# Splits of weights and operands queued on ScalarE behind a visit's last exponential, in an attention loop that runs beside large products

## The chip, the core and the metric

The kernel runs on one core of a Trainium2 chip. The core has a matrix engine (TensorE, PE in the profile), a vector engine (VectorE, DVE), a scalar engine (ScalarE, ACT), GpSimd (POOL) and a sync engine (SyncE, SP) that issues most of the DMAs. Each engine has its own list of instructions and they wait for one another through semaphores. The metric is the device time of one execution in microseconds (us). Three runs of the kernel before took 1274.01, 1275.73 and 1276.46 us, so its median is 1275.73 us.

## What is computed

One layer of a hybrid decoder, for 1024 tokens of width 1024, in float32. After a norm, one wide projection makes all inputs. One branch is a state-space scan (SSD), the other is attention with a forgetting gate; both pass through a product with a matrix of their own, are merged by sigmoid gates, and go through an output product and a norm. The part that matters here is the attention of 16 heads:

```python
def _forgetting_attention(q, k, v, log_f):
    seqlen = q.shape[2]
    scale = ATT_HEAD_DIM ** -0.5
    fcum = jnp.cumsum(log_f, axis=-1)
    outs = []
    for blk in range(seqlen // ATT_BLOCK):
        q0, q1 = blk * ATT_BLOCK, (blk + 1) * ATT_BLOCK
        s = jnp.einsum('bhqd,bhkd->bhqk', q[:, :, q0:q1], k[:, :, :q1]).astype(jnp.float32) * scale
        s = s + fcum[:, :, q0:q1, None] - fcum[:, :, None, :q1]
        ...
        prob = jax.nn.softmax(s, axis=-1)
        outs.append(jnp.einsum('bhqk,bhkd->bhqd', prob.astype(v.dtype), v[:, :, :q1]))
...
merged = jax.nn.sigmoid(g_ssm) * p_ssm + jax.nn.sigmoid(g_att) * p_att
out = jnp.einsum('bld,de->ble', merged, w_out)
```

## The kernel before

All large products are computed by a scheme of Strassen's kind: each pair of output units is made of seven smaller products, called steps 1 to 7. A step is twelve matmuls of 128x128 by 128x512 in two halves of six. There are twelve because each operand is kept as two pieces, a high piece that is rounded and a low piece that is the rest, and high times high, high times low and low times high are summed for each of four blocks. The weight of a step has the tile `wop`. `Pair.split` makes it: ScalarE copies the raw block (or a sum of blocks) into the high piece (L349), and VectorE subtracts that from the raw block into the low piece (L350). The other operand, one of x0 to x6, has tiles such as x5h (high) and x5l (low); `Operands.split` makes them block by block, the high on ScalarE (L275, L278) and the low on VectorE (L276, L279). A low piece always needs its high piece.

`Stream` holds the list of all steps and runs it in halves. At each step `Stream.ahead` calls `prepare` for the step three places further on, which splits its weight, and `Operands.some` fetches and splits operand blocks of pairs still to come.

The attention runs in 48 visits, eight pairs of heads times six groups of rows and keys, and halves of the product stream are run in between so that TensorE has work while the softmax is computed. Each visit `m` goes in this order: `scores` (two rounds `u` of twelve matmuls into PSUM tiles s, VectorE's row minimum nm with bias, L1505, and ScalarE's exponential ex, L1509, each four times per visit); `weighted` for the visit before (matmuls into av); `free`; the work deferred from the visit before, such as `second` (x at L1594, then y at L1595, for which y was loaded by a DMA at L1569); a number `ahead` of product halves; `turned` (TensorE transposes the exponentials into PSUM tiles pt; ScalarE, at L1548, or VectorE, at L1546, evacuates them into p); and a number `behind` of halves. The PSUM tiles s and pt share one set of four banks, so the scores of a visit wait for the evacuations of the one before. During `behind` the operand work is held back (`hold`) and done by `release` in the next visit.

The order of each engine's list is set by a scheduler that estimates times. Blocks under `tc.high_priority()` come early, and instructions wrapped in `pin` keep the order in which the program wrote them. `tc.issue_after(i)` gives what is traced inside it an edge in the order of issue behind instruction `i`, on the engine of `i`, without a semaphore.

Other lines named below: L402 (`keep`) and L413 to L419 (`give`) take finished products out of PSUM; L629 and L644 apply tanh to gates, L645 and L1074 continue with them on VectorE; L1413, L1414 normalise; L1457, L1469 and L1470 form the attention output o and zr; L1373 is GpSimd's mask, L1432 a DMA of ScalarE.

Of the kernel before, what the change touches and what calls it, by code (L numbers as in the profile page):

```python
# [11 lines left out]
AF = mybir.ActivationFunctionType  # L12
# [74 lines left out]
def hybrid_layer(ctx: ExitStack, tc, a, out):  # L87

    nc = tc.nc
# [43 lines left out]
    def pin(op):  # L133
        return tc.keep_in_program_order(op)
# [326 lines left out]
    class Stream:  # L461
# [6 lines left out]
        def __init__(self, pairs, double, last):  # L468
            self.pairs = pairs
            for n, p in enumerate(pairs):  # L470
                p.bank, p.other = (pj, "be"[n % 2]), (pjx, "d") if n < double else (pj, "c")

                p.between = n < double or n >= last

            p, q, r = pairs[0:3]
            self.steps = [(p, 1), (q, 1), (p, 2), (q, 2)] + [(p, n) for n in (6, 5, 7, 4, 3)]
            self.steps += [(q, 6), (q, 5), (q, 7), (r, 1), (q, 4), (q, 3)]
            for n in range(2, last):
                p, nxt = pairs[n], pairs[n + 1]
                self.steps += [(p, i) for i in ((2, 6, 5, 7) if n < double else (6, 2, 7, 5))] + [(nxt, 1)]  # L480
                self.steps += [(p, 4), (p, 3)] if n + 1 < last else [(p, 3), (p, 4)]

            a, b, c, d, e, f, g, h = pairs[last:]
            self.steps += [(a, 5), (a, 6), (a, 7), (b, 1), (a, 2), (a, 4), (a, 3)]
            for p, nxt in ((b, c), (c, d), (d, e)):
                self.steps += [(p, 2), (p, 6), (p, 5), (p, 7), (nxt, 1), (p, 4), (p, 3)]
            self.steps += [(f, 1), (e, 2), (e, 6), (e, 5), (e, 7), (f, 2), (e, 4), (e, 3)]
            self.steps += [(f, 6), (f, 5), (f, 7), (g, 1), (f, 4), (f, 3)]
            self.steps += [(g, 2), (g, 6), (g, 5), (g, 7), (h, 1), (g, 4), (g, 3)]
            self.steps += [(h, 6), (h, 5), (h, 7), (h, 2), (h, 3), (h, 4)]  # L490
            self.following = {p: n.ops for p, n in zip(pairs, pairs[1:]) if n.ops is not p.ops}
            self.building = []
            self.chores, self.line = [], []
            self.held = None
            self.count = 0
            self.at = 0
            self.run = None
            self.waiting = []
            self.loads = [(p, names) for p in pairs for names in (("a11", "a12"), ("a21", "a22"))]
            self.loaded = []  # L500
            self.load_next()

        def load_next(self):
            p, names = self.loads.pop(0)
            p.load(names)
            if p.keys[0][0] != "merged":
                self.loaded += [(p, n) for n in names]

        def load_more(self):

# [14 lines left out]
                self.prepare(p, which)  # L525

        def prepare(self, p, which):
            p.prepare(which)
            self.load_more()

        def after(self, halves, fn):
# [3 lines left out]
        def half(self):  # L535
            if self.run is None:
                if self.at == len(self.steps):
                    return False
                p, which = self.steps[self.at]
# [12 lines left out]
            else:  # L552
# [3 lines left out]
                p, which = self.steps[self.at]  # L556
                if p in self.following:
                    ops = self.following[p]
# [4 lines left out]
                self.at += 1  # L563
            for ops in self.building:
                if self.held is None:
                    ops.some()
                else:
                    self.held.append(ops)
            for chores in (self.chores, self.line):
# [16 lines left out]
        def release(self):  # L586
            held, self.held = self.held or [], None
            for ops in held:
                ops.some()

        def do_chores(self):
            while self.chores:
# [734 lines left out]
    with tc.tile_pool(name="att", bufs=1, reuse_waits="tile", side="right") as ap, tc.tile_pool(  # L1327
# [148 lines left out]
        def scores(hp, g, u):  # L1476

            pair, h = GROUPS[g]
            i = pair[u]
# [20 lines left out]
            for e in range(2):  # L1500
                o = ex[:, e, u, 0:w]
                nm = hd.at(hd.nm, i, h, e)
                with tc.high_priority():
                    pin(
                        nc.vector.tensor_tensor_reduce(  # L1505
                            o, s[e][:, 0:w], fb[hp, h][:, e, 0:w], 1.0, 3.0e38, ALU.add, ALU.min, nm
                        )
                    )
                    pin(nc.scalar.activation(o, o, AF.Exp, scale=-1.0, bias=nm, accum_out=hd.at(hd.sm, i, h, e)))  # L1509

        def turned(hp, g, sent):

# [160 lines left out]
        def room(m):  # L1673

            share = weights[m // 6] * rooms[m % 6] if m < 6 * NK - 1 else 1.4
            to = stream.steps.index((ends[4], 6))
            n = round((2 * (to - stream.at) - (stream.run is not None)) * share / left[0])
            left[0] -= share
            if m == 6 * NK - 1:
                return n // 2, n - n // 2  # L1680
            behind = n // 2 if n > 3 else min(max(n - 1, 0), 1)
            return n - behind, behind

        made = []
        for m in range(6 * NK + 1):
# [9 lines left out]
            for hd, which in end(m - 1):  # L1695
                hd.free(which)
            if m == 6 * NK:
                stream.release()
                heads[NK - 1].out(2)
                break  # L1700
# [7 lines left out]
            for hd, which in end(m):  # L1708
                hd.settle(which)
            ahead, behind = room(m)  # L1710
            stream.halves(ahead)

            for hd, which in end(m):
                hd.scale(which)
# [78 lines left out]
```

## Time and profile before

| what | value |
|---|---|
| median of three runs | 1275.73 us |
| time of the profiled execution | 1273.87 us |
| its span | 1272.2 us |
| PE busy | 1246.1 us (98%) |
| VectorE busy | 1012.9 us (80%) |
| ScalarE busy | 794.3 us (62%) |
| GpSimd busy | 319.3 us (25%) |
| granted TensorE clock, mean | 0.999 |
| share of PE in the chain that ended last | 86% |

A line of the profile names the line of the program, the engine, the operation, the tile written and the tiles read, and how many of them; then busy time and the mean of one in ns; then the time for which the engine was idle just ahead of them, and what ended most of it. A line of the timeline starts with the start time and the duration in us; brackets at its end give an idle time before it and what ended it. In a line of waits, the engine and line that waited stand first, then what was waited for, and then the total in us, the number of waits and the longest.

### The profile page before, as it was taken

The numbers are of one execution on the slowest core, as the hardware profiler recorded it, in microseconds if no ns is written. First come the engines' busy times: TensorE is split into PE (matmuls) and PEld (weight loads), VectorE is DVE, ScalarE is ACT, GpSimd is POOL, SyncE is SP. The second block draws the span as 40 slices with busy tenths as digits, with TensorE's granted clock in tenths as the row PEclk, the third lists the DMA queues.
The fourth block names the chain that finished last, engine by engine and source line by source line (L and its number), as shares of the span: only waits on it lengthen the run. The fifth ranks groups of instructions, "written<-read, shape, count | busy, mean of one in ns | idle before, by whom it ended". The sixth has DMA issues, their size and how long they took to land.

```text
span 1272.2 us, 20822 instructions
## 1 busy us (share of the span) xinstructions
PE 1246.1 (98%) x6926; PEld 982.3 (77%) x6926; DVE 1012.9 (80%) x1994; ACT 794.3 (62%) x1737; POOL 319.3 (25%) x322
## 2 busy tenths in 40 slices
PE   5999999999999999999999999999999999999997
PEld 3678888888888888888887777777777777778886
DVE  7988886988888978997767676767789767886975
ACT  7745665556665765566555666666687666844753
POOL 4000440013400241115102124223112212356062
PEclk9999999999999999999999999999999999999999
DMA  8232452545436533744447576666687657766933
GB/s 300 69 120 76 146 162 88 191 152 182 138 101 215 175 127 117 219 146 140 142 149 252 162 228 212 217 214 218 232 286 263 224 184 249 249 221 199 364 110 105
DMA packets 152236, 233.56 MB, mean 184 GB/s; under 512 B 15201, under 2 KB 60737, under 8 KB 152129
## 3 DMA queue, kind: packets, MB, share of 16 engines
q1 hardware_dynamic: 136064, 196.08, 47.7%
q10 hardware_dynamic: 10560, 18.06, 3.8%
q0 software_dynamic: 5504, 18.09, 3.7%
q8 instruction: 54, 0.88, 0.3%
q14 instruction: 54, 0.43, 0.1%
HBM read 162.99 MB, written 72.34 MB: 185 GB/s over the span
## 4 chain that ended last, share of the span: by engine, by line
PE 86%; DMA 4%; DVE 4%; ACT 4%; issue 1%; SPq 0%; POOL 0%; DVEq 0%; ACTq 0%; POOLq 0%
PE pb L128 36%; PE pc L128 21%; PE pd L128 7%; PE av L128 5%; PE pt L131 5%; PE s L128 5%; PE yps L128 2%; PE st L128 1%; ACT ex L1509 1%; DMA xt<-in_x 1%; PE tr L131 1%; PE tr_v L131 1%; DMA v<-v_dram 1%; PE df L128 1%; DVE wop L350 1%
## 5 line engine op out<-in xcount | busy, mean ns | idle before, releaser
L350 DVE TENSOR_TENSOR wop<-sum,wop 128x512 fp32r<-128x512 f32 x180 | 140.2, 780 | 53.6 <-ACT wop L349 52.6
L349 ACT ACTIVATE wop<-sum 128x512 fp32r<-128x512 f32 x180 | 112.5, 626 | 109.0 <-DVE sum L355 52.4
L1509 ACT ACTIVATE ex<-ex,nm 128x512 f32<-128x512 f32 (+1 forms) x192 | 116.2, 606 | 71.9 <-DVE nm L1505 71.6
L402 ACT ACTIVATE s<-pb 128x512 f32<-128x512 f32 x144 | 85.3, 593 | 98.2 <-PE pb L128 96.2
L128 PE MATMUL pb<-x0h,wop 128*128 128x512 f32 x384 | 131.5, 399 | 0.0
L128 PE MATMUL pb<-x6h,wop 128*128 128x512 f32 x384 | 129.5, 395 | 1.3 <-ACT s L402 1.3
L128 PE MATMUL pb<-x5h,wop 128*128 128x512 f32 x384 | 130.1, 396 | 0.7 <-ACT s L402 0.7
L350 DVE TENSOR_TENSOR wop<-raw,wop 128x512 fp32r<-128x512 f32 x144 | 105.4, 733 | 31.8 <-ACT wop L349 31.5
L128 PE MATMUL pc<-x3h,wop 128*128 128x512 f32 x384 | 129.8, 396 | 0.5 <-DVE ot L419 0.4
L128 PE MATMUL pc<-x2h,wop 128*128 128x512 f32 x384 | 130.2, 397 | 0.0
L128 PE MATMUL pb<-x4h,wop 128*128 128x512 f32 x384 | 129.1, 395 | 0.0
L1505 DVE CUSTOM_DVE_ANT_0 ex<-s,fb 128x512 f32<-128x512 f32 (+1 forms) x192 | 96.8, 552 | 20.0 <-PE s L128 14.8
L349 ACT ACTIVATE wop<-raw 128x512 fp32r<-128x512 f32 x144 | 89.7, 623 | 14.7 <-PE pd L128 6.1
L128 PE MATMUL pd<-x1h,wop 128*128 128x512 f32 x288 | 96.3, 394 | 0.0
L128 PEld LDWEIGHTS pb<-x6h,wop 128*128 128x128 f32 x384 | 72.1, 188 | 18.6 <-issue 2.0
L128 PEld LDWEIGHTS pb<-x5h,wop 128*128 128x128 f32 x384 | 72.1, 188 | 18.4 <-issue 2.0
L128 PEld LDWEIGHTS pb<-x0h,wop 128*128 128x128 f32 x384 | 72.6, 189 | 17.6 <-issue 2.9
L128 PEld LDWEIGHTS pc<-x3h,wop 128*128 128x128 f32 x384 | 72.1, 188 | 17.7 <-issue 1.5
L128 PEld LDWEIGHTS pc<-x2h,wop 128*128 128x128 f32 x384 | 72.1, 188 | 17.4 <-issue 2.4
L128 PEld LDWEIGHTS pb<-x4h,wop 128*128 128x128 f32 x384 | 72.1, 188 | 16.7 <-issue 1.9
L211 POOL TENSOR_TENSOR wd<-wd 128x256 f32<-128x256 f32 x32 | 32.4, 1011 | 205.0 <-DMA wd<-in_wo 135.0
L131 PE MATMUL pt<-ident,ex 128*128 128x128 f32 x576 | 75.1, 273 | 2.0 <-ACT ex L1509 1.4
(318 smaller groups left out, 2993.6 us busy)
## 6 DMA issues: line engine op xcount, KB each, us to landing
raw<-in_wu SPq DMA_DIRECT2D x128, 256.0 KB
csb<-cs_dram SPq DMA_DIRECT2D x32, 256.0 KB
q<-q_dram SPq DMA_DIRECT2D x32, 256.0 KB
k<-k_dram SPq DMA_DIRECT2D x16, 512.0 KB
fb<-f_dram SPq DMA_DIRECT2D x16, 512.0 KB
rb<-st_dram SPq DMA_DIRECT2D x48, 128.0 KB
wd<-in_wo SPq DMA_DIRECT2D x40, 128.0 KB
xt<-in_x SPq DMA_DIRECT2D x8, 512.0 KB
```

Of the source, the lines that this page charges most:

```text
L128: return tc.keep_in_program_order(nc.tensor.matmul(*args, **kw))
L131: return tc.keep_in_program_order(nc.tensor.transpose(out_, in_, idn))
L211: pin(nc.gpsimd.tensor_tensor(t[out_], t[a_], t[b_], ALU.subtract))
L349: nc.scalar.activation(op[:, 0], src, AF.Copy)
L350: nc.vector.tensor_tensor(op[:, 1], src, op[:, 0], ALU.subtract)
L402: nc.scalar.activation(s, ps, AF.Copy)
L1505: nc.vector.tensor_tensor_reduce(o, s[e][:, 0:w], fb[hp, h][:, e, 0:w], 1.0, 3.0e38, ALU.add, ALU.min, nm)
L1509: pin(nc.scalar.activation(o, o, AF.Exp, scale=-1.0, bias=nm, accum_out=hd.at(hd.sm, i, h, e)))
```

## The change

The last exponential of a visit is remembered in `state["exp"]`. While the `ahead` halves of a visit are run, `stream.front` is that instruction. With `front` set, `prepare` and `Operands.some` are traced inside `tc.issue_after(front)`, so ScalarE's part of the weight splits and operand splits is issued behind the visit's last exponential. VectorE's low pieces are not bound to it themselves, but they need the highs. At all other times `front` is None and nothing is different. `release` gets the same context, but `front` is None when it is called.

```diff
@@ class Stream @@
+            self.front = None
...
+        def behind(self):
+
+            return nullcontext() if self.front is None else tc.issue_after(self.front)
...
         def prepare(self, p, which):
-            p.prepare(which)
+            with self.behind():
+                p.prepare(which)
             self.load_more()
...
             for ops in self.building:
                 if self.held is None:
-                    ops.some()
+                    with self.behind():
+                        ops.some()
                 else:
                     self.held.append(ops)
...
         def release(self):
             held, self.held = self.held or [], None
             for ops in held:
-                ops.some()
+                with self.behind():
+                    ops.some()
@@ scores @@
-                    pin(nc.scalar.activation(o, o, AF.Exp, scale=-1.0, bias=nm, accum_out=hd.at(hd.sm, i, h, e)))
+                    state["exp"] = pin(
+                        nc.scalar.activation(o, o, AF.Exp, scale=-1.0, bias=nm, accum_out=hd.at(hd.sm, i, h, e))
+                    ).ins
@@ loop over visits @@
             if m == 6 * NK:
+                stream.front = None
                 stream.release()
...
             ahead, behind = room(m)
+            stream.front = state["exp"]
             stream.halves(ahead)
+            stream.front = None
```

TensorE's list is the same before and after. On ScalarE and VectorE splits move in 23 visits. In the lists below, ISA rows that write nm are the row minima, and lines that are left out only read out their sums. After the change the program's lines are 8 to 10 further down (L1505 is L1513, L1509 is L1518, L1546 is L1556, L1548 is L1558, L1595 is L1605).

The first place is VectorE in visit 12, before:

```order
L1470 TENSOR_TENSOR zr_7688<-o_7978 128x256
L350 TENSOR_TENSOR wop_8191<-sum_8189,wop_8191 128x512
L1505 ISA ex_6721,nm_8147<-s_8153,fb_7799 128x512
...
L1505 ISA ex_6721,nm_8147<-s_8154,fb_7799 128x512
...
L1505 ISA ex_6721,nm_8147<-s_8165,fb_7799 128x384
```

And VectorE in visit 12 after the change:

```order
L1478 TENSOR_TENSOR zr_7688<-o_7978 128x256
L1513 ISA ex_6721,nm_8147<-s_8153,fb_7799 128x512
...
L1513 ISA ex_6721,nm_8147<-s_8154,fb_7799 128x512
...
L1513 ISA ex_6721,nm_8147<-s_8165,fb_7799 128x384
...
L1513 ISA ex_6721,nm_8147<-s_8166,fb_7799 128x384
...
L350 TENSOR_TENSOR wop_8191<-sum_8189,wop_8191 128x512
```

The low piece of one weight has moved from ahead of the four minima to behind them.

The second place is visit 30. ScalarE before, where th_10221 is an evacuation of PSUM and x5h are highs of an operand:

```order
L402 ACTIVATE s_10154<-pb_10107 128x512
L349 ACTIVATE wop_10202<-raw_9495 128x512
L278 ACTIVATE x5h_9985<-x5l_9986 128x512 x2
L1509 ACTIVATE ex_6721,sm_10157<-ex_6721,nm_10156 128x512 x2
L1509 ACTIVATE ex_6721,sm_10157<-ex_6721,nm_10156 128x384
L413 ACTIVATE th_10221<-pb_9615 128x512
L349 ACTIVATE wop_10268<-raw_9493 128x512
L1509 ACTIVATE ex_6721,sm_10157<-ex_6721,nm_10156 128x384
L278 ACTIVATE x5h_9985<-x5l_9986 128x512 x2
```

ScalarE in visit 30 after the change:

```order
L402 ACTIVATE s_10154<-pb_10107 128x512
L1518 ACTIVATE ex_6721,sm_10157<-ex_6721,nm_10156 128x512 x2
L1518 ACTIVATE ex_6721,sm_10157<-ex_6721,nm_10156 128x384 x2
L278 ACTIVATE x5h_9985<-x5l_9986 128x512 x2
L349 ACTIVATE wop_10202<-raw_9495 128x512
L278 ACTIVATE x5h_9985<-x5l_9986 128x512 x2
L413 ACTIVATE th_10221<-pb_9615 128x512
L349 ACTIVATE wop_10268<-raw_9493 128x512
```

The four exponentials now follow one another, and two weight highs, two operand highs and the evacuation at L413 stand behind them.

VectorE in visit 30 before, from the third minimum on (o, x and y are the deferred attention output, p_10261 an evacuation of transposed exponentials):

```order
L350 TENSOR_TENSOR wop_10202<-raw_9495,wop_10202 128x512
L279 TENSOR_TENSOR x5l_9986<-x5l_9986,x5h_9985 128x512
L1505 ISA ex_6721,nm_10156<-s_10174,fb_9755 128x384
...
L1505 ISA ex_6721,nm_10156<-s_10175,fb_9755 128x384
...
L279 TENSOR_TENSOR x5l_9986<-x5l_9986,x5h_9985 128x512
L1457 TENSOR_TENSOR o_10194<-av_10066,zr_10123 128x512
L1594 TENSOR_TENSOR x_9860<-zr_9628,x_9860 128x512
L350 TENSOR_TENSOR wop_10268<-raw_9493,wop_10268 128x512
L1595 TENSOR_TENSOR y_10125<-x_9860,y_10125 128x512
L1546 COPY p_10261<-pt_10239 128x512
L279 TENSOR_TENSOR x5l_9986<-x5l_9986,x5h_9985 128x512 x2
```

VectorE in visit 30 after the change:

```order
L1513 ISA ex_6721,nm_10156<-s_10175,fb_9755 128x384
...
L1465 TENSOR_TENSOR o_10194<-av_10066,zr_10123 128x512
L1604 TENSOR_TENSOR x_9860<-zr_9628,x_9860 128x512
L1605 TENSOR_TENSOR y_10125<-x_9860,y_10125 128x512
L279 TENSOR_TENSOR x5l_9986<-x5l_9986,x5h_9985 128x512
L1556 COPY p_10261<-pt_10239 128x512
L279 TENSOR_TENSOR x5l_9986<-x5l_9986,x5h_9985 128x512
L350 TENSOR_TENSOR wop_10202<-raw_9495,wop_10202 128x512
L279 TENSOR_TENSOR x5l_9986<-x5l_9986,x5h_9985 128x512 x2
L350 TENSOR_TENSOR wop_10268<-raw_9493,wop_10268 128x512
L1513 ISA ex_6721,nm_10156<-s_10284,fb_10129 128x512
```

Two weight lows and two operand lows have moved from ahead of y to between y and the next visit's first minimum (s_10284). Between the minima of that next visit two x3 lows now stand that stood ahead of them, and two visits later the copy of p at L1546 has the step of L1074 ahead of it that was behind it.

The third place is VectorE behind the last visit. Before:

```order
L1469 TENSOR_TENSOR o_12056<-o_12056,rb_12138 128x512
L279 TENSOR_TENSOR x3l_12003<-x3l_12003,x3h_12002 128x512
L1470 TENSOR_TENSOR zr_11721<-o_12056 128x256
L279 TENSOR_TENSOR x3l_12003<-x3l_12003,x3h_12002 128x512
L1594 TENSOR_TENSOR x_11960<-zr_11721,x_11960 128x512
L1074 TENSOR_SCALAR th_12206<-th_12082,th_12206 128x512
L350 TENSOR_TENSOR wop_12246<-raw_11936,wop_12246 128x512
L1595 TENSOR_TENSOR y_12092<-x_11960,y_12092 128x512
L276 TENSOR_SCALAR x4l_11777<-x_11960,x4h_11776 128x512
L1457 TENSOR_TENSOR o_12269<-av_12169,zr_12217 128x512
L276 TENSOR_SCALAR x2l_12135<-x2l_12135,x2h_12134 128x512 x2
```

And behind the last visit after the change, where the row ahead of these is the same o_12056:

```order
L279 TENSOR_TENSOR x3l_12003<-x3l_12003,x3h_12002 128x512
L350 TENSOR_TENSOR wop_12186<-sum_12184,wop_12186 128x512
L1478 TENSOR_TENSOR zr_11721<-o_12056 128x256
L279 TENSOR_TENSOR x3l_12003<-x3l_12003,x3h_12002 128x512 x2
L1082 TENSOR_SCALAR th_12206<-th_12082,th_12206 128x512
L1604 TENSOR_TENSOR x_11960<-zr_11721,x_11960 128x512
L350 TENSOR_TENSOR wop_12246<-raw_11936,wop_12246 128x512
L1605 TENSOR_TENSOR y_12092<-x_11960,y_12092 128x512
L350 TENSOR_TENSOR wop_12293<-raw_11411,wop_12293 128x512
L1465 TENSOR_TENSOR o_12269<-av_12169,zr_12217 128x512
L276 TENSOR_SCALAR x2l_12135<-x2l_12135,x2h_12134 128x512 x3
L276 TENSOR_SCALAR x4l_11777<-x_11960,x4h_11776 128x512
```

The last low of operand x4 now has the weight low wop_12186 (which stood ahead of the last visit's minima), one more x3 low, wop_12293, o_12269 and three x2 lows between o_12056 and itself that were ahead of o_12056 or behind it.

## The prediction

> **What bounds the kernel now.** I read the windows by stage first, then the groups, then the waits of the attention stage, and last the timelines of single visits. The 48 visits lie between about 682 and 1112 us.
>
> ```profile
> core 0: us, PE busy (x) PEld busy (x) DVE busy (x) ACT busy (x) POOL busy (x), PEclk, DMA share, GB/s
> 682.00:1112.00 430.00, 427.33 (x2860) 323.76 (x2860) 321.69 (x849) 292.77 (x740) 110.51 (x144) 1.00 0.67 224
> 940.00:980.00 40.00, 38.34 (x237) 27.57 (x232) 36.88 (x86) 32.58 (x80) 7.38 (x11) 1.00 0.79 270
> 1112.00:1123.00 11.00, 9.97 (x47) 6.99 (x46) 10.99 (x20) 8.21 (x17) 1.51 (x2) 1.00 0.74 235
> ...
> L1509 ACT ACTIVATE ex<-ex,nm 128x512 f32<-128x512 f32 (+1 forms) x192 | 116.2, 606 | 71.9 <-DVE nm L1505 71.6
> ...
> PEld s L128 <- ACT p L1548: 7.6, 22, 0.5
> PEld pt L131 <- ACT ex L1509: 2.8, 5, 1.2
> PE pt L131 <- ACT ex L1509: 1.4, 3, 0.9
> ```
>
> PE bounds the stage: it is idle for 2.7 of 430 us. ScalarE has slack (293 of 430 us), VectorE less, and around 960 us and at 1112 to 1123 us almost none. An exponential that starts late waits for the row minimum (nm) of VectorE, 71.6 of its 71.9 us, not for the split ahead of it on ScalarE. All that PE waits for exponentials is a few us. So an earlier exponential can gain a few us at most, and what VectorE now does later may cost as much. I therefore went through the visits in which the change moves something. There are 23 of them; in most, PE reaches its transposes (pt) after the last exponential and the move is hidden.
>
> **Gain in visits 12 and 27.** Both lose time at pt.
>
> ```profile
> 787.90 0.68 DVE L350 TENSOR_TENSOR wop<-sum,wop 128x512 fp32r<-128x512 f32 x1
> ...
> 791.53 0.27 PE L131 MATMUL pt<-ident,ex 128*128 128x128 f32 x1
> 792.01 0.77 PE L131 MATMUL pt<-ident,ex 128*128 128x128 f32 x5 [0.21 <-ACT ex L1509]
> ...
> 918.54 0.69 DVE L350 TENSOR_TENSOR wop<-sum,wop 128x512 fp32r<-128x512 f32 x1
> 920.37 0.69 DVE L279 TENSOR_TENSOR x0l<-x0l,x0h 128x512 fp32r<-128x512 f32 x1
> ...
> 923.01 2.45 PE L131 MATMUL pt<-ident,ex 128*128 128x128 f32 x16
> ...
> 963.13 1.91 PE L131 MATMUL pt<-ident,ex 128*128 128x128 f32 x16
> ```
>
> In visit 12 one transpose starts 0.48 us after the one before it, against about 0.11 (1.91 us less the last one's 0.27, over 15 steps): a stall of 0.37. The weight's low half that VectorE did at 787.90, ahead of the four reductions, now stands behind them, so the exponentials end 0.6 us sooner and the stall goes. In visit 27 sixteen transposes take 2.45 us against 1.91: 0.54 us. Here a low half and two operand lows leave the space ahead of and between the reductions. I take -0.37 - 0.54 = **-0.9 us**; the ends are 0 and -0.9, and I take the full value since the VectorE work that delayed the reductions is really gone from there. What is late next is the moved weight; its first use by PE is in the third step to come, and a step is 12 matmuls at 0.23 us or 2.8 us. That, with the visits' own work between, is its cover, and I cost its lateness at nothing; without the cover a split would cost its own 0.6 us per visit.
>
> **Visit 0 gains nothing.** It has the longest pt stalls of the early visits, but not from the split.
>
> ```profile
> 684.10 0.63 ACT L644 ACTIVATE th<-th 128x512 f32<-128x512 f32 x1 [0.99 <-DMA za_dram<-th]
> ...
> 686.10 0.72 ACT L1509 ACTIVATE ex<-ex,nm 128x512 f32<-128x512 f32 x1 [1.37 <-DVE nm L1505]
> ...
> 689.72 0.58 ACT L1548 ACTIVATE p<-pt 128x512 f32<-128x512 f32 x1
> ...
> 690.94 1.43 PE L128 MATMUL s<-k,q 64*128 64x512 f32 x10
> ```
>
> The reductions wait behind the gate's tanh th, which waits for a DMA that frees its tile; that stays. But ScalarE runs without a gap from the last exponential to the evacuations (p), and the split (0.52 us, two of them take 1.04 in the rows 971.32 and 972.36 below) now lies between. The evacuations end 0.52 later, and the scores at 690.94 need their banks. Ends 0 and +0.52; some of it is inside the time that twelve score matmuls take, so **+0.3 us**.
>
> **Visits 30 to 33.** This is the largest pt stall, and the place where most is moved: two x5 highs, two weights, and a PSUM evacuation (L413) on ScalarE; two weight lows and two x5 lows on VectorE.
>
> ```profile
> 944.70 0.39 SPq L1569 DMA_DIRECT2D y<-ya_dram  x1
> ...
> 952.49 0.27 PE L131 MATMUL pt<-ident,ex 128*128 128x128 f32 x1
> 953.69 0.55 PE L131 MATMUL pt<-ident,ex 128*128 128x128 f32 x3 [0.93 <-ACT ex L1509]
> ...
> 952.84 0.68 DVE L1594 TENSOR_TENSOR x<-zr,x 128x512 f32<-128x512 f32 x1
> 953.44 0.68 DVE L350 TENSOR_TENSOR wop<-raw,wop 128x512 fp32r<-128x512 f32 x1
> 954.39 0.69 DVE L1595 TENSOR_TENSOR y<-x,y 128x512 f32<-128x512 f32 x1 [0.27 <-DMA y<-ya_dram]
> ...
> 958.01 0.68 DVE L1505 CUSTOM_DVE_ANT_0 ex<-s,fb 128x512 f32<-128x512 f32 x1
> ...
> 964.80 1.53 ACT L1548 ACTIVATE p<-pt 128x512 f32<-128x512 f32 x3
> ...
> 967.70 0.91 PE L128 MATMUL s<-k,q 64*128 64x256 f32 x12
> ...
> 969.03 0.41 DVE L1505 CUSTOM_DVE_ANT_0 ex<-s,fb 128x256 f32<-128x256 f32 x1
> ...
> 971.32 1.14 ACT L278 ACTIVATE x6h<-x6l 128x512 fp32r<-128x512 f32 x2
> 972.36 1.14 ACT L275 ACTIVATE x2h<-x2l 128x512 fp32r<-128x512 f32 x2
> ...
> 976.78 0.42 DVE L1546 COPY p<-pt 128x256 f32<-128x256 f32 x1
> ...
> 977.26 0.96 PE L128 MATMUL s<-k,q 64*128 64x512 f32 x5 [0.38 <-DVE p L1546]
> ```
>
> A full VectorE step is 0.60 us from start to start (952.84 to 953.44). First the gain: the four reductions follow one another, PE's transposes lose their stall of 1.1 us and two small ones, and PE is 1.6 us earlier. It can't keep it. Without the two weights and the two x5 lows VectorE is through o and x at about 951.7, but y still waits for its DMA until 954.39: VectorE stands 2.7 us, in order, with the work that was pulled out from before y now behind it. Behind y come seven steps (four x5 lows, the evacuation COPY, two weights), 4.2 us, so visit 31's first reduction starts at about 959.2 instead of 958.0, and with two x3 lows between its four reductions the last ends at 962.8 instead of 960.4 (958.01 and four steps). Its exponentials end 2.1 us later, and so the three evacuations (964.80 before) begin at about 966.9. Of these 2.1 us some 1.3 are covered, since the next scores came at 967.70, after the evacuations had ended at 966.3, and PE was early. The rest goes on: visit 32's reductions start about 0.9 us later than 969.03, ScalarE's x6 and x2 highs behind them too, and the copy of p on VectorE, for which PE's scores already waited at 977.26, is 0.9 later and has one more step ahead of it (th of L1074, 0.6). That makes **+1.5 us** at that wait, everything from visit 30 on included. The ends: +0.5 if y lands as early as VectorE reaches it, so that only the added step counts; +2.3 if almost none of the 2.4 us by which visit 31's last reduction slips is caught up. -1.6 would need all of this covered.
>
> One weight low on that path ran slower than the others.
>
> ```profile
> 965.80 2.62 POOL L1373 TENSOR_TENSOR fb<-fb,far 64x256 f32<-64x256 f32 x2
> ...
> 967.88 1.08 DVE L350 TENSOR_TENSOR wop<-raw,wop 128x512 fp32r<-128x512 f32 x1
> ```
>
> It took 1.08 us instead of 0.68 while GpSimd's masks ran. After the change it starts at about 969.3, behind their end at 968.4; I count it at the normal 0.60, which is in the +1.5. [...]
>
> **The tail (visit 47 and the steps behind it).** No later work is left to absorb anything.
>
> ```profile
> 1107.43 1.16 DVE L350 TENSOR_TENSOR wop<-sum,wop 128x512 fp32r<-128x512 f32 x1
> ...
> 1111.61 0.69 DVE L1469 TENSOR_TENSOR o<-o,rb 128x512 f32<-128x512 f32 x1 [0.33 <-DMA rb<-st_dram]
> ...
> 1116.17 0.68 DVE L276 SCALAR_TENSOR_TENSOR x4l<-x,x4h 128x512 fp32r<-128x512 f32 x1
> ...
> 1119.15 0.39 PE L128 MATMUL pb<-x4l,wop 128*128 128x512 f32 x1
> ...
> 1120.45 0.50 PE L128 MATMUL pb<-x5h,wop 128*128 128x512 f32 x1 [0.69 <-ACT s L402]
> ```
>
> The low half at 1107.43 and one x3 low go from before the wait for rb (1111.61) to behind it. The time that they leave is no gain, since rb does not come sooner. From 1111.61 VectorE then works through o, three x3 lows, three weights, zr (0.34), th, x, y, o and three x2 lows before the last x4 low: 14 steps of 0.60 and the short one, 8.7 us, so it runs from about 1120.35 to 1121.0. PE asks for it at 1119.15 in the trace, and at about 1119.05 with the x3 lows in their new order (which cost it as much as before, within 0.1 us). The stall is 1.95 us: **+2.0 us**, and VectorE has no idle time there (10.99 of 11 us busy) in which to catch up. Ends: 0 if the x2 lows go ahead of an x4 low that is needed later than I read, and +2.6 with one more step ahead of it.
>
> **Sum.** -0.9 + 0.3 + 1.5 + 2.0 = +2.9 us. The profiled execution took 1273.87 us, so 1276.8; the median of the runs shown is 1.86 above it, which gives **1278.6 us**. A difference of 0.2% (2.55 us, about what a measurement of this kernel can tell from no change) ends at 1278.28.
>
> **Rivals.** (a) *Faster: the losses are covered.* y's load is the only late thing in visit 30; if it lands when VectorE gets there, and the last x4 low is in time, then -0.9 and up to -1.6 of visit 30 remain: 1273.2 to 1274.8. It decides at y's landing: up to about 953.2 (958.0 less y's own step and the seven behind it, 4.8 us) visit 31's reductions begin no later than now. For it: VectorE waited only 0.27 us for y. Against it: it came 2.7 us later than VectorE will ask for it, and its issue on SP's queue at 944.70 is ahead of everything that moves. Chance 0.20. (b) *Only one of the two losses is real:* +0.9 to +1.4, so 1276.6 to 1277.1, within 0.2%. Chance 0.14. (c) *More slower:* evacuations later in the visits where ScalarE has no gap between the last exponential and p, which shows as more than the 7.6 us of scores waiting for p. In 22 waits 0.1 us more each, +2.2, makes 1280.8, and 0.2 more each 1283. Against it: in most moved visits ScalarE is idle for longer than one split before p. Chance 0.16. [...] (d) *The change doesn't act*, since exponentials wait for nm: the rows of visits 12 and 27 speak against it, as the moved low halves free VectorE too.
>
> **How the numbers follow.** My forecast has 0.50, with 1277.3 to 1280.5 as its own range; 0.36 of it lies over 1278.28, 0.14 under. Slower: 0.36 + 0.16 = 0.52. Same: 0.14 + 0.14 + 0.04 of (a) = 0.32. Faster: the rest of (a), 0.16, for which visits that I count at nothing would have to add a little. The range goes from (a) with most of its gain, 1273.4, to (c) with nearly 0.2 us a wait, 1282.4.
>
> **What would show it.** Right: no pt stall in visits 12, 27 and 30; visit 0 as before; a wait of VectorE for y of over 2 us near 952; scores of visit 33 waiting over 1 us for a copy of p; PE waiting about 2 us for x4l near 1119. Wrong: y waited for under 1 us, no wait for x4l, or waits of scores for p over 10 us in all.

## The result and the profile after

The changed kernel takes 1284.91 us (median of six runs, 1283.12 to 1287.7) against 1276.1 us before (six runs, 1274.01 to 1279.27). The ratio is 1.0067 with a 95% interval of 1.0053 to 1.0081: slower by some 8.6 us. The prediction was 1278.6 us, in a range up to 1282.4: the direction was right, and the size was about a third of the real one.

The profiled execution took 1285.15 us with a span of 1283.4 us, which is 11.2 us more than the span before. These are its windows by stage and around two places, in the same columns as before:

```profile
686.00:1118.00 432.00, 426.55 (x2843) 324.23 (x2842) 322.52 (x845) 287.96 (x737) 107.77 (x144) 1.00 0.66 221
1118.00:1140.00 22.00, 18.85 (x73) 13.56 (x71) 20.11 (x31) 12.56 (x25) 5.20 (x5) 0.84 0.62 202
...
830.49:833.90 3.41, 2.12 (x24) 1.67 (x26) 3.08 (x11) 3.04 (x10) 0.00 (x0) 1.00 0.42 162
833.90:837.31 3.41, 3.41 (x16) 2.25 (x13) 0.38 (x2) 0.83 (x5) 0.00 (x0) 0.50 0.33 105
1124.03:1127.44 3.41, 1.54 (x7) 0.98 (x6) 3.41 (x7) 0.68 (x2) 0.00 (x0) 1.00 0.72 213
1127.44:1130.86 3.42, 2.73 (x7) 1.64 (x7) 3.39 (x6) 2.65 (x6) 0.84 (x1) 0.50 0.98 320
1130.86:1134.27 3.41, 3.41 (x10) 2.64 (x9) 2.88 (x4) 0.54 (x2) 1.04 (x2) 0.50 0.62 209
1134.27:1137.68 3.41, 3.41 (x17) 2.78 (x16) 2.63 (x4) 2.15 (x5) 1.16 (x1) 1.00 0.35 125
```

PE's idle time in the attention rises from 2.7 to 5.5 us. What the prediction's sum has no term for is the column PEclk: in one stretch near 834 us and in two near 1127 us the granted clock is 0.50, and PE, though busy, starts the products' matmuls 0.42 us apart there instead of 0.23. Before, it was 1.00 from 20 us on but for the last 3 us.

The groups of the exponentials and the waits of the attention stage and the tail:

```profile
L1518 ACT ACTIVATE ex<-ex,nm 128x512 f32<-128x512 f32 (+1 forms) x192 | 115.9, 605 | 73.6 <-DVE nm L1513 73.1
...
PEld s L128 <- ACT p L1558: 11.7, 27, 1.8
PE s L128 <- ACT p L1558: 3.0, 4, 1.5
PE s L128 <- DVE p L1556: 2.0, 3, 1.2
PE pb L128 <- DVE x4l L276: 1.9, 1, 1.9
PEld pt L131 <- ACT ex L1518: 0.5, 1, 0.5
```

The exponentials wait for the minima as long as before (73.1 us against 71.6). The waits for exponentials are nearly gone (0.5 us of weight loads and 0.2 us of PE, against 2.8 and 1.4). In their place stand the scores' waits for evacuations p, 3.0 and 2.0 us of PE against 0.2 and 0.4, and the wait for the last x4 low.

Since PE's list is the same in both kernels, each matmul can be set against itself. The time by which it starts later in the changed kernel grows like this:

| place | start before to start after, growth (us) | predicted |
|---|---|---|
| up to 682 us, where both kernels have one order | +1.7 | 0 |
| visit 0 | 0.0 | +0.3 |
| visit 12 | -0.5 | -0.4 |
| visit 16, 829 to 833 us | +3.4 | 0 |
| visit 27, up to the scores of visit 30 | +0.3 | -0.5 |
| visits 30 to 33, from visit 30's transposes on | 0.0 | +1.5 |
| visits 43 to 46 | +1.0 | 0 |
| tail, 1119 to 1124 us | +5.0 | +2.0 |
| behind it | +0.3 | 0 |

The first row is no effect of the change. Among the kernels below, all with that same order, the growth by 682 us was between 0.1 and 2.0 us. The profiled execution of before is also one of its quickest (1273.87 us against medians of 1275.5 to 1277.1). So some 9 us of the 11.2 belong to the change.

**Visits 27 and 30.** What PE gained at the transposes it gave back at once. In visit 27 it gained 0.6 us and lost 0.9 by visit 30's scores, before anything that moved in visit 30 could act; e12 below, which leaves visit 30 as it was, shows the same steps. In visit 30 it gained 1.8 us at the transposes and lost 1.5 at the next scores, of which the rest of these scores made up 0.5:

```profile
956.58 1.14 ACT L278 ACTIVATE x5h<-x5l 128x512 fp32r<-128x512 f32 x2
...
960.34 0.36 ACT L1558 ACTIVATE p<-pt 128x256 f32<-128x256 f32 x1
...
960.74 1.92 PE L128 MATMUL s<-k,q 64*128 64x512 f32 x11 [1.45 <-ACT p L1558]
```

The moved highs and the evacuation L413 keep ScalarE from 956.58 until its copies p begin, and PE's scores wait for these. A last 0.9 us was lost at the scores of visit 33, which waited 1.15 us for a copy of p on VectorE, as predicted.

**Visit 16.** Before, on GpSimd, VectorE, ScalarE and PE (GpSimd's additions of masks, a step of the second weight sum, the evacuation th of a product, the copies p, the next scores):

```profile
823.97 3.72 POOL L1373 TENSOR_TENSOR fb<-fb,far 64x256 f32<-64x256 f32 x4 [5.30 <-DVE nm L1505]
...
825.00 0.68 DVE L379 TENSOR_TENSOR raw<-raw 128x512 f32<-128x512 f32 x1
826.44 0.69 DVE L417 TENSOR_TENSOR th<-pc,s 128x512 f32<-128x512 f32 x1 [0.76 <-POOL fb L1373]
...
827.86 0.83 ACT L1548 ACTIVATE p<-pt 128x256 f32<-128x256 f32 x2
...
829.29 0.90 PE L128 MATMUL s<-k,q 64*128 64x256 f32 x12
```

After:

```profile
824.42 3.22 POOL L1381 TENSOR_TENSOR fb<-fb,far 64x256 f32<-64x256 f32 x4 [4.69 <-DMA raw<-in_wu]
827.72 1.61 POOL L211 TENSOR_TENSOR th<-x,th 128x512 f32<-128x512 f32 x1
...
826.08 1.04 DVE L350 TENSOR_TENSOR wop<-sum,wop 128x512 fp32r<-128x512 f32 x1 [0.88 <-ACT wop L349]
827.15 1.05 DVE L355 TENSOR_TENSOR sum<-sum,raw 128x512 f32<-128x512 f32 x1
828.23 1.66 DVE L379 TENSOR_TENSOR raw<-raw 128x512 f32<-128x512 f32 x1
829.81 0.68 DVE L417 TENSOR_TENSOR th<-pc,s 128x512 f32<-128x512 f32 x1
...
830.52 0.63 ACT L637 ACTIVATE th<-th 128x512 f32<-128x512 f32 x1 [1.60 <-DVE th L417]
831.22 0.83 ACT L1558 ACTIVATE p<-pt 128x256 f32<-128x256 f32 x2
...
831.62 0.80 PE L128 MATMUL s<-k,q 64*128 64x256 f32 x7 [1.21 <-ACT p L1558]
832.58 0.55 PE L128 MATMUL s<-k,q 64*128 64x128 f32 x5 [0.15 <-ACT p L1558]
```

One weight moved here. Its low waits for the high, which is now behind the exponentials, and the two sums that stand behind it in VectorE's list come later too. Before, the low was done ahead of GpSimd's four additions, and the two sums ran beside the first two of them: the sums took 0.69 and 0.68 us, and it was these two additions that were slow, 1.04 and 1.14 us against 0.67 for the other two. After, low and sums start when GpSimd is already at its third addition, and now VectorE is slow: 1.04, 1.05 and 1.66 us instead of 0.69 or less. The evacuation th on VectorE starts 3.4 us later by the traces' own times (1.1 us of it was there before this visit), ScalarE's tanh waits for it, and the copies p stand behind the tanh on ScalarE. So the scores wait.

**The tail.** VectorE and PE after the change:

```profile
1126.42 0.69 DVE L276 SCALAR_TENSOR_TENSOR x4l<-x,x4h 128x512 fp32r<-128x512 f32 x1
...
1124.66 0.63 PE L128 MATMUL pb<-x4h,wop 128*128 128x512 f32 x2
1127.16 0.58 PE L128 MATMUL pb<-x4l,wop 128*128 128x512 f32 x1 [1.87 <-DVE x4l L276]
1127.54 0.63 PE L128 MATMUL pb<-x4h,wop 128*128 128x512 f32 x1
1128.86 0.79 PE L128 MATMUL pb<-x5h,wop 128*128 128x512 f32 x1 [0.69 <-ACT s L402]
```

The wait for x4l is 2.05 us longer than before, as predicted. But from 1127.44 on the clock is 0.50, and the next eleven or so matmuls start 0.42 instead of 0.23 us apart, which costs another 2.8 us.

### The profile page after: what moved, and what is told of

Read it like the earlier page. It is cut to its first block, busy times and chain, and to the rows that moved or that the text cites. A ratio compares the mean times of both kernels' runs of the same rounds, so it can differ in the third digit from the quotient of the medians.

```text
span 1283.4 us, 20813 instructions
## 1 busy us (share of the span) xinstructions
PE 1251.4 (98%) x6926; PEld 986.3 (77%) x6926; DVE 1014.8 (79%) x1994; ACT 791.0 (62%) x1737; POOL 314.1 (24%) x322
## 4 chain that ended last, share of the span: by engine, by line
PE 74%; DVE 9%; DMA 7%; ACT 6%; issue 3%; SPq 1%; POOL 0%; DVEq 0%; ACTq 0%; POOLq 0%
PE pb L128 32%; PE pc L128 17%; PE pd L128 6%; PE av L128 5%; PE s L128 4%; PE pt L131 4%; PE yps L128 2%; DVE wop L350 2%; DMA raw<-in_wu 1%; ACT ex L1518 1%; DVE sum L355 1%; ACT wop L349 1%; DMA xt<-in_x 1%; PE st L128 1%; PE tr L131 1%
## 5 line engine op out<-in xcount | busy, mean ns | idle before, releaser
L1518 ACT ACTIVATE ex<-ex,nm 128x512 f32<-128x512 f32 (+1 forms) x192 | 115.9, 605 | 73.6 <-DVE nm L1513 73.1
L1513 DVE CUSTOM_DVE_ANT_0 ex<-s,fb 128x512 f32<-128x512 f32 (+1 forms) x192 | 95.7, 553 | 18.7 <-PE s L128 13.6
L211 POOL TENSOR_TENSOR wd<-wd 128x256 f32<-128x256 f32 x32 | 32.2, 1007 | 202.9 <-DMA wd<-in_wo 100.9
L128 PE MATMUL pb<-x4l,wop 128*128 128x512 f32 x192 | 75.2, 392 | 2.2 <-DVE x4l L276 1.9
```

The lines of the kernel that those rows point to most:

```text
L128: return tc.keep_in_program_order(nc.tensor.matmul(*args, **kw))
L211: pin(nc.gpsimd.tensor_tensor(t[out_], t[a_], t[b_], ALU.subtract))
L1513: nc.vector.tensor_tensor_reduce(o, s[e][:, 0:w], fb[hp, h][:, e, 0:w], 1.0, 3.0e38, ALU.add, ALU.min, nm)
```

## The experiments

Theory A: the loss sits in a few places where VectorE's work is done later than before, and in some of them the idle time of PE brings down its clock. The rivals were a loss spread over all visits (B), and stalls alone with no part of the clock (C). In all but e5 to e8 the edit is one line that limits the change to some visits; the rest of the engines' order stays. e7 and e8 add an edit to such a line. The first four ran beside the kernel before at 1275.64 us (17 runs).

**e1: all visits but the last**

```diff
-            stream.front = state["exp"]
+            stream.front = state["exp"] if m != 47 else None
```

> The change in all visits but the last (47). Theory A, the loss sits in two places and is doubled by the clock: the wait for the last x4 low (2.05 us) and the half clock behind it (11 matmuls x 0.2 and what follows, about 2.8 us) are gone, so about 4.9 us less than the changed kernel: 1280 us, granted clock 1.00 between 1120 and 1140 us. Theory B, the loss is spread over many visits: within 1 us of the changed kernel's 1284.9. Theory C, only the stalls cost and half clocks come as often without the change: about 2 us less, 1282.9.

Measured: 1282.03 us, ratio 1.0056 (1.0037 to 1.0074). In the trace the tail is clean: no wait for x4l, clock 1.00 from 1120 to 1140 us. But a half clock now came at 982 us, behind the scores of visit 33, and cost 1.6 us. The median fell by 2.9 us, not by 4.9, and half clocks like this one may be why. Visit 16 waited 1.9 us with no half clock behind it. The tail is a cause; where a half clock falls differs from trace to trace.

**e2: the last visit alone**

```diff
-            stream.front = state["exp"]
+            stream.front = state["exp"] if m == 47 else None
```

> The change in the last visit (47) alone. Theory A: before plus 2 us of waiting for x4l plus about 2.8 us of half clock, 1281 us; the half clock comes in whole stretches of 3.4 us, so 2 to 5 us more. Theory B: within 1 us of before, 1276. Theory C: before plus 2 us, 1278, with the clock at 1.00.

Measured: 1278.67 us, ratio 1.0022 (1.0012 to 1.0033), 3.0 us over before. In the trace PE's start at the tail slips by 2.06 us at x4l and by 1.7 us in one stretch of half clock behind it:

```profile
1119.60:1123.01 3.41, 1.79 (x7) 1.18 (x8) 3.38 (x7) 1.71 (x4) 0.00 (x0) 1.00 0.98 294
1123.01:1126.42 3.41, 3.41 (x10) 2.64 (x9) 3.41 (x5) 1.49 (x3) 2.17 (x2) 0.50 0.77 262
1126.42:1129.83 3.41, 3.41 (x16) 2.80 (x15) 3.25 (x6) 2.12 (x4) 1.09 (x1) 1.00 0.59 211
```

Ten matmuls instead of sixteen in a stretch in which PE is busy throughout: this agrees with A, and not with B. The median is nearer to the 1278 us of C than to the 1281 of A, since one stretch was halved and not two; that the clock has a part is read from the trace. In this trace, with the order of before in visit 12, the pt stall of that visit was gone as well. So the stall that I saw there in the profile of before does not come with the order each time.

**e3: all visits but 16**

```diff
-            stream.front = state["exp"]
+            stream.front = state["exp"] if m != 16 else None
```

> The change in all visits but 16. Theory A: the wait of the scores for late evacuations near 830 us (1.9 us) and the half clock behind it (1.5 us) are gone, 3.4 us less than the changed kernel, 1281.5 us. Theory B: within 1 us of 1284.9. Theory C: 1.9 us less, 1283.

Measured: 1282.5 us, ratio 1.0055 (1.004 to 1.007), 2.4 us below the changed kernel. Nothing was lost at 829 us. This trace had half clocks at 1110.79 and 1127.85 us, which cost 1.6 and 1.7 us; the first, behind a wait of 0.5 us, is an extra one and hides part of the gain.

**e4: visit 16 alone**

```diff
-            stream.front = state["exp"]
+            stream.front = state["exp"] if m == 16 else None
```

> The change in visit 16 alone, one weight's split. Theory A: before plus 1.9 us of scores waiting, and 1.5 us of half clock where its stretch falls as in the changed kernel: 1278 to 1279.5 us. Theory B: within 1 us of before, 1276. Theory C: before plus 1.9 us, 1278, with the clock at 1.00.

Measured: 1278.95 us, ratio 1.0027 (1.0015 to 1.0038), 3.3 us over before, from one moved weight. The trace loses 3.4 us between 829 and 833 us, 1.9 of it waiting and the rest in a stretch of half clock at 834.58. This agrees with A.

**e5 and e6: weights alone, and operands alone.** In e5 the operand splits are left free, in e6 the weight splits. These two and the next two ran beside before at 1275.54 us (25 runs).

```diff
@@ e5 @@
-                    with self.behind():
-                        ops.some()
+                    ops.some()
@@ e6 @@
-            with self.behind():
-                p.prepare(which)
+            p.prepare(which)
```

> Only the splits of weights are bound behind the last exponential; operand splits are left free. Theory A (the weight lows, queued late on VectorE in visit 16 and at the tail, carry the loss): the same as the changed kernel, 1283.5 to 1285.5 us, with the stalls near 830 and at x4l. Rival (the operand splits of visits 27, 30, 43 and 47 carry it): within 2 us of before, 1276 to 1278.

> Only the operand splits are bound behind the last exponential; weight splits are left free. Theory A: within 1 us of before, 1275 to 1277 us, no stall near 830 and none at x4l. Rival (the operand splits carry the loss): 1283 or more.

Measured: e5 1285.2 us, ratio 1.0068 (1.0043 to 1.0092); e6 1279.24 us, ratio 1.0027 (1.0014 to 1.0039). e5 doesn't separate the two kinds: in its trace the order of PE, VectorE, ScalarE and GpSimd and of the DMA issues is that of the changed kernel, operand splits included. So it is the changed kernel once more, and repeats its loss; its trace had one more half clock, at 962.88 us, behind the scores of visit 31. In e6 neither the stall near 830 nor the one at x4l is there, so these two need the weights' edges. But e6 costs 3.7 us, which neither side expected: in visits 30 to 33 its trace loses 1.3 us, with VectorE waiting 1.4 us for y, and a half clock at 1109 us costs 1.6, behind a wait of 0.6 us at the scores of visit 47. How much operand splits alone would cost, no run shows, since weight lows moved with them in visit 30 of e6.

**e7: visit 16 without the masks.** As e4, but GpSimd's four mask additions of that visit are left out, so that later scores there are not masked.

```diff
-            if g in (1, 3, 4):
+            if g in (1, 3, 4) and m != 16:
                 mask(hp, {1: 5, 3: 3, 4: 1}[g])
-            if g == 4 and more:
+            if g == 4 and more and m != 16:
                 mask(hp + 1, 7)
```

> As the change in visit 16 alone, but GpSimd's four mask additions of that visit are left out (so later scores there are not masked). Theory A1 (the three VectorE steps behind the moved high, 1.04, 1.05 and 1.66 us, are slow because they run beside the masks): they take about 0.6 each, the product's evacuation on VectorE comes about 2 us sooner, the scores wait under 0.3 us, no half clock near 834: 1275 to 1276 us. Rival A2 (the order alone delays the evacuations; one split of 0.5 us and a late low): the wait stays at 1 us or more, 1277.5 to 1279.

Measured: 1276.01 us, ratio 1.001 (0.9999 to 1.0022), 2.9 us below e4. VectorE and PE in its trace:

```profile
825.58 0.69 DVE L350 TENSOR_TENSOR wop<-sum,wop 128x512 fp32r<-128x512 f32 x1 [0.88 <-ACT wop L349]
826.31 0.69 DVE L355 TENSOR_TENSOR sum<-sum,raw 128x512 f32<-128x512 f32 x1
827.03 0.69 DVE L379 TENSOR_TENSOR raw<-raw 128x512 f32<-128x512 f32 x1
827.64 0.68 DVE L417 TENSOR_TENSOR th<-pc,s 128x512 f32<-128x512 f32 x1
...
829.86 1.10 PE L128 MATMUL s<-k,q 64*128 64x256 f32 x12
```

The order is that of e4 on VectorE, ScalarE and PE. Without GpSimd's additions the steps take 0.69 us, th is in time, the scores slip by 0.2 us instead of 1.9, and there is no half clock. So the order alone does not make the loss of visit 16. It makes it by laying VectorE's low and sums beside GpSimd's work, where these three steps took 1.04, 1.05 and 1.66 us in e4.

**e8: the last visit alone, with PE's wait filled.** Eight matmuls into a PSUM bank that nothing reads stand ahead of the matmul that waits for x4l.

```diff
                 for n, (w, m) in enumerate(((0, xh), (0, xl), (1, xh))):
+                    if k == KH - 1 and n == 1 and which == 6 and "fill" in fin:
+                        idle = fin.pop("fill")
+                        for d in range(8):
+                            mm(idle, op[:, 0, 0, :], xh[:, 0, :], start=d == 0, stop=d == 7, skip_group_check=True)
...
+    pjf = ctx.enter_context(tc.tile_pool(name="pjf", bufs=1, space=PSUM, reuse_waits="tile", side="right"))
+    fin["fill"] = pjf.tile([P, HALF], F32, name="idle")
     while stream.half():
```

> As the change in visit 47 alone, with eight more matmuls into an unused PSUM bank just ahead of the matmul that waits for the last x4 low, 1.8 us of work in a wait of 2.05 us. Theory A (the clock is halved because PE was idle): the wait shrinks to about 0.2 us of idle time, the clock stays at 1.00 between 1118 and 1130 us, and the time is 1.7 us below the change in visit 47 alone (1278.7), 1277. Rival (the half clock has another cause): clock 0.5 as before, 1278.7.

Measured: 1278.37 us, ratio 1.0019 (1.0009 to 1.003); the medians of e2 and e8 can't be told apart. In the trace:

```profile
1122.02 1.97 PE L128 MATMUL idle<-x4h,wop 128*128 128x512 f32 x8
1124.05 0.50 PE L128 MATMUL pb<-x4l,wop 128*128 128x512 f32 x1
...
1124.40:1127.80 3.40, 2.71 (x12) 1.96 (x11) 3.37 (x7) 2.98 (x6) 0.00 (x0) 1.00 0.96 316
```

The wait for x4l is as long as in e2 (2.05 us), the clock stays at 1.00 and nothing more is lost behind it, where e2 lost 1.7 us. That is the step expected: with this wait unfilled the changed kernel and e2 have a half clock next behind it, at 1127.44 and 1123.01 us, and this one has none. Over 1120 to 1140 us the mean clock was 0.83 in the changed kernel, 0.91 in e2, e3 and e5, and 1.00 here. But ahead of it this run lost 1.0 us at the x3 lows, where VectorE waited 0.63 us for rb, which it did not wait for in e2. So the one trace supports the clock's part, and the medians do not settle it.

**e9, e10, e11: the two gains, visit 30, and visits 42 to 44.** Beside before at 1276.79 us (29 runs).

```diff
@@ e9 @@
+            stream.front = state["exp"] if m in (12, 27) else None
@@ e10 @@
+            stream.front = state["exp"] if m == 30 else None
@@ e11 @@
+            stream.front = state["exp"] if m in (42, 43, 44) else None
```

> The change in visits 12 and 27 alone, the two with the gain predicted. Theory A: the pt stalls there go, 0.4 us and 0.4 to 0.5 us, nothing is given back, and the clock stays at 1.00: 0.9 us below before, about 1274.7 us, which is less than a measurement can tell; the trace of the profiled run shows the two steps. Rival: what VectorE does later in these visits costs as much behind them (scores waiting for p), 1275.6 or more.

Measured: 1276.88 us, ratio 1.0008 (0.9994 to 1.0021). No gain. In the trace visit 12 ends 0.4 us later than in the trace of before, and visit 27 gains 0.6 us at its transposes and loses 1.0 up to the scores of visit 30: the rival.

> The change in visit 30 alone. My prediction had +1.5 us from visit 30 to 33 with VectorE waiting 2.7 us for y. In the changed kernel's trace y came early and the four visits cost 0.4 us; with operand splits alone VectorE waited 1.4 us for y and they cost 1.8. Theory A: the cost follows the wait for y, 0.4 us without one and 1.5 to 2 us with 1.4 us or more: 1276 to 1277.5, and one half-clock stretch if the scores of visit 33 wait over 1 us. Rival: the cost is the same whether y waits or not (order of p's copy alone).

Measured: 1278.58 us, ratio 1.0012 (1.0 to 1.0023), hardly clear of none. VectorE and PE in its trace:

```profile
955.47 0.69 DVE L1605 TENSOR_TENSOR y<-x,y 128x512 f32<-128x512 f32 x1 [1.67 <-DMA y<-ya_dram]
...
979.28 0.50 PE L128 MATMUL s<-k,q 64*128 64x512 f32 x1 [1.13 <-ACT p L1558]
980.93 0.95 PE L128 MATMUL s<-k,q 64*128 64x512 f32 x5 [1.15 <-DVE p L1556]
```

With y waited for by 1.67 us the four visits cost 1.6 us up to these scores, close to the +1.5 of the prediction, and a half clock at 982.5 us cost 1.5 more. In the changed kernel y came without a wait and they cost 0.0. Three traces (0, 1.4 and 1.67 us of waiting in the changed kernel, e6 and e10; 0.0, 1.3 and 1.6 us of loss) agree with A. With the scores of visit 30 as the start, the figures of 0.4 and 1.8 in the expectation become 0.0 and 1.3; the rest was visit 27's.

> The change in visits 42 to 44 alone. The changed kernel, the one without 47 and the one without 16 each lost 0.9 to 1.4 us between 1086 and 1105 us, at scores that wait for late evacuations; I did not predict that. Theory A: the moved weight of visit 43, queued on ScalarE and VectorE ahead of visit 44's evacuations, causes it: +0.9 to +1.4 us there, 1276.5 to 1277. Rival: it comes from the lateness carried in from visit 30 or from DMA times: under 0.3 us there.

Measured: 1277.92 us, ratio 1.001 (0.9999 to 1.0022), not clear of none. The trace slips by 1.7 us between 1074 and 1097 us. The 0.5 us of it at transposes near 1074 is no sign of the change, since e7, with the order of before there, lost 0.8 at the same place. The other 1.2 us were lost at two rounds of scores near 1086 and 1096. There the traces of the changed kernel, e1, e3 and e5 lose 0.9 to 1.2 us too, e6 loses 0.7, and e2, e4, e7, e8, e10 and e12 lose nothing. So this loss comes from the moved splits of these visits and not from lateness carried in. In e10 and e11 PE also waited 1.51 us for an x3 low at the tail, where the order is that of before (0.35 us there), behind an rb that VectorE waited 0.8 us for. Both medians came out about 1 us above what was expected, and the tail, which varies by more than 1 us from trace to trace, may be why.

**e12: all visits but these.** Beside before at 1277.09 us (17 runs).

```diff
-            stream.front = state["exp"]
+            stream.front = state["exp"] if m not in (16, 30, 42, 43, 44, 47) else None
```

> The change in all visits but 16, 30, 42, 43, 44 and 47, the places in which loss was found. Theory A (late VectorE work in these few places, and the half clock that two of them bring, is all of the loss): within 1 us of before, 1275.5 to 1277.5 us, and no half clock before the end. Rival (a share is spread over the other seventeen visits): 2 us or more above before.

Measured: 1276.74 us, ratio 1.0009 (0.9996 to 1.0021); its span was 1272.4 us against 1272.2 before. Its windows:

```profile
682.00:1112.00 430.00, 426.81 (x2858) 323.71 (x2857) 324.43 (x848) 290.01 (x739) 110.58 (x144) 1.00 0.67 224
1112.00:1123.00 11.00, 9.93 (x48) 6.99 (x47) 10.98 (x19) 8.62 (x18) 1.09 (x2) 1.00 0.69 226
```

No half clock, and PE about as idle as before. With the six visits left out, the change in the other seventeen costs and gains nothing that these runs can measure, though the interval alone would leave room for up to 2.7 us, and the trace is of the quickest of the twelve runs. The parts speak for A too: alone, visit 47, visit 16, visit 30 and visits 42 to 44 came out 3.0, 3.3, 1.8 and 1.1 us over before, 9.2 together against 8.8 for the whole. So all that can be found of the loss is in these six. No version was faster than the kernel before.

## Why the prediction was right in direction and wrong in size

- **"An earlier exponential can gain a few us at most, and what VectorE now does later may cost as much."** Right, and the core of it: the pt stalls went and the scores' waits for p grew, as the waits above show.
- **"In most, PE reaches its transposes (pt) after the last exponential and the move is hidden."** This is the step that failed first. I tested each visit for what stood in front of PE's transposes, and for the lateness of the moved weight. I did not test what stands behind the moved low on VectorE, and took the rest of the lateness at nothing. In visit 16 it holds up an evacuation that ScalarE waits for ahead of its copies, and the copies gate the next scores: 1.9 us there, and 0.9 to 1.2 us in visits 43 to 46, against 0 in the sum. My rival (c) had this mechanism, but put it in visits without a gap on ScalarE, and said that ScalarE's idle time covers it. In visit 16 ScalarE was idle because it waited for VectorE.
- **The masks.** I counted a slow VectorE step beside GpSimd once, as a gain (visit 32's weight leaving GpSimd's time; it did, and took 0.68 us against 1.08 before). I did not look for steps that move into such a time. In visit 16 the three slowed steps took 3.75 us. In e7, without the additions, they took 0.69 us each and the scores slipped by 0.2 us instead of 1.9, so GpSimd's work beside them decides this.
- **The tail, +2.0.** The stall was sized right: 2.05 us in the changed kernel, in e2 and in e3. The term left out what follows it, 1.7 us of half clock in e2 and 2.8 in the changed kernel.
- **The clock.** No term of the sum stands for it, and this is the dearest single omission. In the profile of the changed kernel three stretches of 3.41 us ran at 0.50, which cost 1.5 us at visit 16 and 2.8 us at the tail, nearly half of the loss of some 9 us. The sum has a stall of 1.95 us at the tail and prices nothing behind it, but a half clock came behind a wait of 1.21 us among small matmuls and behind one of 1.87 us, in stretches in which PE was busy for 62 and 45%. The profile of before had 1.00 throughout these stages and could not show it.
- **Visits 30 to 33, +1.5.** Close where y came late (e10, +1.6), wrong for the changed kernel's own run (0.0), where y did not have to be waited for. The 2.7 us of waiting came from one landing time in one trace. The copy of p behind the step of L1074 cost 0.9 us, as forecast. But of the 1.6 us by which I had PE earlier most went at visit 31's scores, which waited for p behind the moved highs on ScalarE. I did not look for that wait there.
- **Visit 0, +0.3.** 0.0 in this trace: the waits at pt shrank by 0.7 and the next scores lost as much. I had no gain and a small loss, where there were both, and their sum nearly right. That is luck.
- **Visits 12 and 27, -0.9.** Visit 12's stall comes and goes with one and the same order of that visit: it is gone in the traces of e2, e7 and e8, and longer in those of e4 and e10. Visit 27's gain is real at the transposes and is given back by the scores of visit 30. e9 shows no gain. I should have taken the end at 0.
- **My own signs.** Of those for "wrong" two came: y was hardly waited for, and the scores waited for p for more than 10 us in all (PE's weight loads alone waited 11.4 us for ScalarE's copies, 682 to 1112 us). Of those for "right" the wait for x4l and that of visit 33's scores came.

## What to carry to other kernels

When work is queued behind an instruction, look behind the place where it lands, on every engine that follows it: who waits for the instructions that now stand after it, and what other engine's work it will lie beside. A PE wait like that of visit 16, in a kernel that PE bounds, should get a second price with a chance of its own: its 1.9 us cost 3.4 us in the changed kernel and e4, and 1.9 in e1. A stall of a few tenths seen in one trace is no term of a sum before a second trace has it too.

## What the runs showed of the hardware

Half clocks came in whole stretches of 3.41 us: one from 833.90 and two from 1127.44 us in the changed kernel (293.5 us apart, 86 stretches), one from 834.58 us in e4 and one from 1123.01 us in e2. Each change of the granted clock came a whole number of stretches after the one before it: 238, 1, 85, 2 and 43 in the changed kernel (812.37, 3.41, 290.13, 6.83 and 146.77 us) and 366 before (1249.28 us). Where one begins did not follow the program: the matmul that waited for x4l started 0.28 us ahead of the half clock in the changed kernel (1127.16) and 2.48 us ahead of it in e2 (1120.53). Nor did the length of the wait alone decide whether one came. In the changed kernel waits of 1.21 us (to 831.62) and 1.87 us (to 1127.16) were followed by one, and waits of 1.45 us (to 960.74) and 1.15 us (to 982.17) were not. The last stretch at 1.00 ahead of a half clock had PE busy for 62 and 45% there and 52% in e2; the stretches of the waits without one had 74, 84 and 66%. What decides it, these runs do not show.

In visit 16 VectorE's low and sums overlapped GpSimd's additions and L211. In both profiles the one of two that began second ended 0.53 to 0.55 us after the other had ended (1.14 or 1.15 us where it was L211), whichever engine it was on; an overlap of 0.01 us is left aside. Before, VectorE's two sums began ahead of an addition each and kept 0.69 and 0.68 us, and the additions took 1.04 and 1.14 us. In the changed kernel the low came behind the third addition, the fourth addition behind the low, the first sum behind the fourth addition, L211 behind the first sum, and the second sum behind L211: 1.04, 1.05 and 1.66 us on VectorE. In e4 the same three steps took 1.04, 1.05 and 1.66 us too.
